# Sample attention of a hybrid decoder: both batches of a pair in one array pass, keys and values of both in one load

## The chip, the core and the metric

The kernel runs on one core of one Trainium2 chip. The metric is the time of one execution on the device in microseconds (us): the median of several runs. A profiled execution gives the trace from which the views below come; its span is the time from the first to the last instruction of the program.

## The reference

One step of a decoder layer for a prompt of 2048 tokens and for 8 running samples with 8 new tokens each. Both go through the same input projection, an attention group, an SSD group (Mamba-2), an output projection and a squared-ReLU MLP; all in f32. The change is in the attention of the samples. Each new token attends to its window buffer of 2048 cached keys and to the new keys, in three dilated groups which are combined by their log-sum-exp:

```python
def dilated_group_sample(q, k_ext, v_ext, dilation, n_keys, n_past):
    t = q.shape[1]
    idx = n_past + jnp.arange(t)[:, None] - dilation * jnp.arange(n_keys + 1)[None, :]
    valid = idx >= 0
    idx = jnp.maximum(idx, 0)
    kg, vg = k_ext[:, idx], v_ext[:, idx]
    scores = jnp.einsum('btkgd,btjkd->btkgj', q, kg, preferred_element_type=jnp.float32)
    scores = jnp.where(valid[None, :, None, None, :], scores, NEG_BIG)
    lse = jax.nn.logsumexp(scores, axis=-1)
    p = jnp.exp(scores - lse[..., None])
    o = jnp.einsum('btkgj,btjkd->btkgd', p.astype(vg.dtype), vg)
    return o, lse
```

There are 8 query heads on 4 key-value heads of 64 features, so 64 query rows (8 heads times 8 tokens) for each sample.

## The kernel before, in words

The program first does the projections and the prompt's attention, then, from about a third of the span on, the output projection (`out`, tile ps_o) and the MLP (`up`, ps_up; `down`, ps_dn) of four tiles T of 512 prompt tokens. Each f32 product of the MLP is made of three matmuls (L1124, L1126, L1127): the weight tile `raw_m` is loaded by SP (L896), split by ACT into `wm_h` (L899) and by DVE into `wm_l` (L900). There are 4 `raw` buffers and 6 of each half.

Beside tile T's MLP runs the preparation of tile T + 1, a generator (`work`) that is stepped by a plan: `tick` is called once for each `down` step, and PLAN[T] says how many steps of the generator must be done by then. For T = 1 these are the SSD work of tile 2 and then the sample attention (`sample_att`), in 26 planned steps. The generator only records instructions; a scheduler with a simulated clock then sets the order in which each engine gets them, and the engines take their instructions in that order. Copies of the key and value caches to the outputs (`shift`) run on SP too.

`sample_att` goes over 4 pairs of samples (bp). The 1280 cached keys that any of the three groups uses are gathered on the host into `kTs` (features on partitions) and `vTs` (keys on partitions); the mask `sk` holds the logarithm of how often a key counts. A pair has 128 query rows: sample be = 0 in rows 0 to 63, be = 1 in rows 64 to 127, and within a sample the two head pairs pr in 32 rows each. Its steps:

- scores (tile ps_ss): for each be, in chunks of 512, 512 and 256 keys and for each pr, a load `kts` (L1531, 3 buffers) and a matmul (L1534) with the 32 query rows as weights, so that the result lies in 32 PSUM partitions and takes 32 columns of the array; the last chunk has the 8 new keys `kn` too (L1536). DVE adds the mask and writes `Sx` (L1538), 64 partitions at a time;
- softmax over all 128 rows: maximum (L1541), exp on ACT (L1542), sum (L1544);
- transposes of the weights into 11 blocks PT (tile ps_pt, L1554);
- values (tile ps_po): for each be, five loads `vts` of two key blocks (L1566, 2 buffers) and ten matmuls (L1568), each with the 64 columns of PT of that sample as weights and 256 value features moving, then one with the new values `vn` (L1570). All add up in 64 partitions of one PSUM bank;
- the result is scaled (L1573), transposed (ps_ao, L1576) and copied into `mixA`.

The generator yields six times for a pair.

Of the kernel before, what the change touches and what calls it, by code (L numbers as in the profile page):

```python
# [9 lines left out]
F32 = mybir.dt.float32  # L10
F32R = mybir.dt.float32r
AF = mybir.ActivationFunctionType
ALU = mybir.AluOpType
# [4 lines left out]
P = 128  # L18
# [5 lines left out]
DB, DT = 8, 8  # L24
# [9 lines left out]
NEWP = 1280  # L34
# [72 lines left out]
def build(nc, tc, ctx, I, O, dbg=None, stop=None):  # L107
# [595 lines left out]
    def att_b(G_, T):  # L703
# [11 lines left out]
        for grp, A in enumerate(T.A):  # L715
            V, dV = (T.V1, T.dV1) if grp == 0 else (T.V2, T.dV2)
            for half in range(2):
# [23 lines left out]
                for prev in (0, 1):  # L741
                    for e in range(2):
# [743 lines left out]
def sample_att(nc, tc, I, O, psm, ident, qs_s, ks_s, smx, kn_s):  # L1486
    NT = DB * DT
    with ExitStack() as cx:
        sp = cx.enter_context(tc.tile_pool(name="smp", bufs=1, reuse_waits="tile"))
        mix = sp.tile([P, 4, NT], F32, name="mixA")  # L1490

        qz = sp.tile([P, 2, DB, 2, 2, DT], F32, name="qz")
        nc.vector.memset(qz, 0.0)
        kn = sp.tile([P, 2, NT], F32, name="kn")
# [8 lines left out]
        sk = sp.tile([P, NEWP + DT], F32, name="sk")  # L1503
# [11 lines left out]
        mixa = mix.rearrange("p (a j) n -> p a j n", a=2)  # L1515
        for bp in range(DB // 2):
            Sx = sp.tile([P, NEWP + DT], F32, tag="Sx", name="Sx", bufs=1)
            V = []
            for be in range(2):
                b = 2 * bp + be  # L1520
                vn = sp.tile([DT, 256], F32, tag="vn", name="vn", bufs=2)
                nc.sync.dma_start(vn, O["vnew"][b * DT:(b + 1) * DT])
                V.append(vn)
                r0 = 64 * be
                for n0 in range(0, NEWP + DT, 512):
                    n1 = min(n0 + 512, NEWP + DT)
                    ps = psm("ps_ss")
                    m1 = min(n1, NEWP)
                    for pr in range(2):
                        kt = sp.tile([P, 512], F32, tag="kts", name="kts", bufs=3)  # L1530
                        nc.sync.dma_start(kt[:, :m1 - n0], I["kTs"][b][:, pr, n0:m1])  # L1531
                        lq = qz[:, pr, b].rearrange("p e j t -> p (e j t)")
                        o = ps[r0 + 32 * pr:r0 + 32 * pr + 32]
                        nc.tensor.matmul(o[:, :m1 - n0], lq, kt[:, :m1 - n0], start=True, stop=True, skip_group_check=True)  # L1534
                        if n1 > NEWP:
                            nc.tensor.matmul(o[:, m1 - n0:n1 - n0], lq, kn[:, pr, b * DT:(b + 1) * DT], start=True, stop=True,  # L1536
                                             skip_group_check=True)
                    nc.vector.tensor_tensor(Sx[r0:r0 + 64, n0:n1], ps[r0:r0 + 64, :n1 - n0], sk[r0:r0 + 64, n0:n1], op=ALU.add)  # L1538
                yield
            mx = sp.tile([P, 1], F32, tag="mx", name="mx", bufs=1)  # L1540
            nc.vector.tensor_reduce(mx, Sx, axis=AX.X, op=ALU.max, negate=True)  # L1541
            nc.scalar.activation(Sx, Sx, AF.Exp, bias=mx)  # L1542
# [3 lines left out]
            NK = NEWP // P  # L1546
            PT = []
            for q0 in range(0, NK + 1, 4):
                q1 = min(q0 + 4, NK + 1)
                ps = psm("ps_pt")  # L1550
                pt_ = sp.tile([P, q1 - q0, P], F32, tag="PT", name="PT", bufs=3)
                for q in range(q0, q1):
                    w = P if q < NK else DT
# [5 lines left out]
                    nc.scalar.activation(pt_[:DT, NK - q0], ps[:DT, (NK - q0) * P:(NK - q0 + 1) * P], AF.Copy)  # L1559
            yield  # L1560
            po = psm("ps_po")
            for be in range(2):
                o = po[64 * be:64 * be + 64, :256]
                for j in range(5):
                    v = sp.tile([P, 2, 256], F32, tag="vts", name="vts", bufs=2)
                    nc.sync.dma_start(v, I["vTs"][2 * bp + be][:, 2 * j:2 * j + 2])  # L1566
                    for q in range(2):
                        nc.tensor.matmul(o, PT[2 * j + q][:, 64 * be:64 * be + 64], v[:, q], start=j + q == 0, stop=False,  # L1568
                                         skip_group_check=True)
                nc.tensor.matmul(o, PT[NK][:DT, 64 * be:64 * be + 64], V[be], start=False, stop=True, skip_group_check=True)  # L1570
                yield
            ao = sp.tile([P, 256], F32, tag="ao", name="ao", bufs=1)
            nc.scalar.activation(ao, po[:, :256], AF.Copy, scale=dn)  # L1573
            pt = psm("ps_ao")
# [55 lines left out]
def mix_rows():  # L1630
    a = np.arange(512).reshape(2, 2, 2, 64).transpose(0, 2, 1, 3).ravel()
    return np.concatenate([a, 512 + np.arange(512)])
# [21 lines left out]
def prep(x):  # L1654
    x = {n: np.asarray(a) for n, a in x.items()}
    A = {}
# [6 lines left out]
    w = x["w_in"][0]  # L1663
# [12 lines left out]
    j = np.arange(P)  # L1676
# [8 lines left out]
    idx, A["sk"] = sample_keys()  # L1685
    ck, cv_ = x["cache_k"][0].reshape(DB, 2048, 256), x["cache_v"][0].reshape(DB, 2048, 256)
    A["ck"], A["cv"] = ck, cv_
    A["kTs"] = ck[:, idx].reshape(DB, NEWP, 2, P).transpose(0, 3, 2, 1)
    A["vTs"] = cv_[:, idx].reshape(DB, NEWP // P, P, 256).transpose(0, 2, 1, 3)
    A["wout"] = mtiles(x["w_out"][0][mix_rows()], slice(None))  # L1690
    xr = np.zeros((KT, P, 8, NB2), np.float32)
    xr[:, :, :, :BS] = xpT.reshape(KT, P, 8, BS)
# [48 lines left out]
```

## Time and profile before

| | |
|---|---|
| median of 3 runs | 2750.95 us (2749.98 to 2755.09) |
| profiled execution | 2750.84 us |
| its span | 2749.1 us |
| outside the span | 1.7 us |
| mean granted TensorE clock | 0.978 |
| sample attention, first to last row on TensorE | 1643 to 1992 us |

In the views, PE is TensorE, PEld its weight loads, DVE VectorE, ACT ScalarE, POOL GpSimd, SP SyncE, and SPq the queue of instructions on SP that issue loads. A timeline row gives start, duration, engine, line, operation, out<-in, the rows and columns of the array in use (128\*32 is 128 rows, 32 columns), partitions x elements, and how many of them stand behind each other. Durations of matmuls overlap, since they are pipelined: what one costs is read from start to start. An f32 matmul stands as two records. A row of the chain of waits has start, duration and what the chain went through. A row of the waits has the waiting engine and line, the releaser, the total, the number of times and the longest.

### The profile page before, as it was taken

To read this page: it belongs to the slowest core of one execution; us is meant where nothing else is said; L and a number is where in the kernel's file an instruction comes from. 1 tells how busy PE (TensorE), PEld (TensorE's weight loads), DVE (VectorE), ACT (ScalarE), POOL (GpSimd) and SP (SyncE) were. 2 spreads that over 40 slices of the span, in tenths; PEclk is the share of its full clock that TensorE was granted. 3 is DMA by queue.
4 is the path that set the end of the run, shared out by engine and by line. 5 is a ranking of instruction groups with operands and counts; after the bars stand their busy time and mean duration, and the time that the engine had idled before them with its cause. 6 is when DMAs were issued, how large, how long until landed. Compare 5 with 4: busy or idle time off the path is not lost.

```text
span 2749.1 us, 42001 instructions
## 1 busy us (share of the span) xinstructions
PE 2630.7 (96%) x15318; PEld 2284.9 (83%) x15318; DVE 1660.8 (60%) x2921; ACT 1146.1 (42%) x2203; POOL 474.3 (17%) x406
## 2 busy tenths in 40 slices
PE   7999789989956999999999999999999999999998
PEld 7999789989955778888888876666688889999998
DVE  6444356887677546777467874444487764554555
ACT  5444235465543424544444442333254434333333
POOL 2222034645522100110201100020010003000000
PEclk9999899999987999999999999999999999999999
DMA  7766767886693635443574544456464434533332
GB/s 258 200 210 214 207 203 214 232 241 196 216 251 99 191 128 174 152 150 119 165 234 153 159 158 147 147 191 209 123 201 146 153 103 153 165 101 108 105 99 85
DMA packets 343327, 464.57 MB, mean 169 GB/s; under 512 B 39744, under 2 KB 219392, under 8 KB 342080
## 3 DMA queue, kind: packets, MB, share of 16 engines
q1 hardware_dynamic: 299376, 425.24, 50.2%
q10 hardware_dynamic: 43744, 36.65, 4.1%
q8 instruction: 121, 1.98, 0.3%
q14 instruction: 86, 0.70, 0.1%
HBM read 366.25 MB, written 129.09 MB: 180 GB/s over the span
## 4 chain that ended last, share of the span: by engine, by line
PE 70%; DMA 1%; DVE 1%; issue 1%; ACT 1%; POOL 0%; SPq 0%; DVEq 0%; ACTq 0%; POOLq 0%
PE ps_dn L1124 9%; PE ps_dn L1126 9%; PE ps_up L1126 9%; PE ps_dn L1127 9%; PE ps_up L1124 9%; PE ps_up L1127 9%; PE ps_o L1126 2%; PE ps_o L1124 2%; PE ps_o L1127 2%; PE ps_po L1568 1%; PE ps_ss L1534 1%; PE ps_xz L177 1%; PE ps_xz L180 1%; PE ps_xz L181 1%; PE ps_yo L1003 1%
## 5 line engine op out<-in xcount | busy, mean ns | idle before, releaser
L899 ACT ACTIVATE wm_h<-raw_m 128x512 fp32r<-128x512 f32 x576 | 362.2, 630 | 840.1 <-PE ps_dn L1126 480.8
L900 DVE TENSOR_TENSOR wm_l<-raw_m,wm_h 128x512 fp32r<-128x512 f32 x576 | 415.8, 724 | 117.1 <-ACT wm_h L899 105.0
L1124 PE MATMUL ps_dn<-uh,wm_h 128*128 128x512 f32 (+1 forms) x1280 | 458.5, 359 | 0.0
L1124 PE MATMUL ps_up<-xh_m,wm_h 128*128 128x512 f32 (+1 forms) x1280 | 458.0, 358 | 0.0
L1126 PE MATMUL ps_dn<-ul,wm_h 128*128 128x512 f32 (+1 forms) x1280 | 457.1, 357 | 0.0
L1126 PE MATMUL ps_up<-xl_m,wm_h 128*128 128x512 f32 (+1 forms) x1280 | 456.4, 357 | 0.0
L1127 PE MATMUL ps_dn<-uh,wm_l 128*128 128x512 f32 (+1 forms) x1280 | 456.0, 357 | 0.0
L1127 PE MATMUL ps_up<-xh_m,wm_l 128*128 128x512 f32 (+1 forms) x1280 | 455.5, 356 | 0.0
L1244 DVE TENSOR_TENSOR acc<-acc,ps_dn 128x512 f32<-128x512 f32 (+1 forms) x320 | 189.2, 592 | 242.6 <-PE ps_dn L1127 239.4
L1124 PEld LDWEIGHTS ps_dn<-uh,wm_h 128*128 128x128 f32 x1280 | 240.3, 188 | 43.5 <-issue 11.0
L1126 PEld LDWEIGHTS ps_dn<-ul,wm_h 128*128 128x128 f32 x1280 | 240.4, 188 | 39.0 <-issue 6.5
L1127 PEld LDWEIGHTS ps_dn<-uh,wm_l 128*128 128x128 f32 x1280 | 240.5, 188 | 37.5 <-issue 4.1
L1126 PEld LDWEIGHTS ps_up<-xl_m,wm_h 128*128 128x128 f32 x1280 | 240.8, 188 | 37.1 <-issue 4.5
L1127 PEld LDWEIGHTS ps_up<-xh_m,wm_l 128*128 128x128 f32 x1280 | 241.1, 188 | 35.4 <-issue 2.0
L1124 PEld LDWEIGHTS ps_up<-xh_m,wm_h 128*128 128x128 f32 x1280 | 240.9, 188 | 34.3 <-issue 1.2
L1232 DVE SCALAR_TENSOR_TENSOR r<-ps_up,rs 128x512 f32<-128x512 f32 (+1 forms) x160 | 95.5, 597 | 141.0 <-PE ps_up L1127 139.7
L177 PE MATMUL ps_xz<-xq,wh 128*128 128x256 f32 (+1 forms) x512 | 149.1, 291 | 12.9 <-DMA xq<-xn_s 8.2
L1235 DVE TENSOR_TENSOR ul<-r,uh 128x512 fp32r<-128x512 f32 (+1 forms) x160 | 97.0, 606 | 93.0 <-ACT uh L1234 93.0
L180 PE MATMUL ps_xz<-xq,wh 128*128 128x256 f32 (+1 forms) x512 | 148.3, 290 | 0.0
L181 PE MATMUL ps_xz<-xq,wl 128*128 128x256 f32 (+1 forms) x512 | 147.8, 289 | 0.0
L1233 ACT ACTIVATE r<-r 128x512 f32<-128x512 f32 (+1 forms) x160 | 88.8, 555 | 115.1 <-DVE r L1232 114.3
L609 PE MATMUL ps_qk<-qt,kA 128*128 128x256 f32 x300 | 103.5, 353 | 21.3 <-DMA qt<-q_s 14.0
(356 smaller groups left out, 5209.2 us busy)
## 6 DMA issues: line engine op xcount, KB each, us to landing
raw_m<-wup SPq DMA_DIRECT2D x256, 256.0 KB
raw_m<-wdn SPq DMA_DIRECT2D x256, 256.0 KB
xq<-xn_s SPq DMA_DIRECT2D x48, 512.0 KB
am<-o_s SPq DMA_DIRECT2D x128, 128.0 KB
raw_m<-wout SPq DMA_DIRECT2D x64, 256.0 KB
ks<-ck SPq DMA_DIRECT2D x32, 510.0 KB
vs<-cv SPq DMA_DIRECT2D x32, 510.0 KB
xz_s<-ev ACTq DMA_DIRECT2D x96, 128.0 KB
```

Of the source, the lines that this page charges most:

```text
L177: r = nc.tensor.matmul(ps, wh(kk), xh(kk), start=kk == 0, stop=False)
L180: nc.tensor.matmul(ps, wh(kk), xl(kk), start=False, stop=False)
L181: k.zl = nc.tensor.matmul(ps, wl(kk), xh(kk), start=False, stop=kk == KT - 1)
L609: k.mm = nc.tensor.matmul(ov, kt[:, ksl], mv, start=first, stop=False, skip_group_check=True)
L899: k.at["ACT"] = nc.scalar.activation(hi, raw, AF.Copy)
L900: nc.vector.tensor_tensor(lo, raw, hi.bitcast(F32), op=ALU.subtract)
L1124: behind(nc.tensor.matmul(ps, wh[:, kk], xh(kk), start=first and kk == 0, stop=False), after)
L1126: nc.tensor.matmul(ps, wh[:, kk], xl(kk), start=False, stop=False)
L1127: r = nc.tensor.matmul(ps, wl[:, kk], xh(kk), start=False, stop=last and kk == nk - 1)
L1232: nc.vector.scalar_tensor_tensor(r, ps, 0.0, c(X.rs), op0=ALU.max, op1=ALU.mult)
L1235: nc.vector.tensor_tensor(c(ul), r, c(uh).bitcast(F32), op=ALU.subtract)
L1244: k.at["DVE"] = nc.vector.tensor_tensor(h, h, ps, op=ALU.add)
```

## The change

Scores: the two samples of a pair are done chunk by chunk together, five chunks of 256 keys. A `kts` tile holds the chunk for both be and both pr (2 x 2 x 256 columns, 512 KB, one load, 2 buffers), and its four matmuls stand behind each other, with results in the four 32-partition strips of one ps_ss bank. The new keys are added after the last chunk. DVE adds the mask for all 128 partitions at once. Values: `vTs` is laid out by pairs, a `vts` tile holds one key block of both samples (256 KB as before), and the two matmuls of a tile are those of be = 0 and be = 1 for the same key block, with weights in columns 0 to 63 and 64 to 127 and results in two halves of one bank. `vn` of both samples comes in one load into one buffer. The generator still yields six times for a pair. In the changed kernel the lines are L1525 (load kts), L1530 (scores), L1537 (new keys), L1558 (transposes), L1568 (load vts), L1570 (values), L1575 (new values).

```diff
@@ scores @@
-            V = []
-            for be in range(2):
-                b = 2 * bp + be
-                vn = sp.tile([DT, 256], F32, tag="vn", name="vn", bufs=2)
-                nc.sync.dma_start(vn, O["vnew"][b * DT:(b + 1) * DT])
-                V.append(vn)
-                r0 = 64 * be
-                for n0 in range(0, NEWP + DT, 512):
-                    n1 = min(n0 + 512, NEWP + DT)
-                    ps = psm("ps_ss")
-                    m1 = min(n1, NEWP)
+            vn = sp.tile([DT, 2, 256], F32, tag="vn", name="vn", bufs=1)
+            nc.sync.dma_start(vn, O["vnew"].rearrange("(p e t) d -> p t e d", e=2, t=DT)[bp])
+            KC = 256
+            for n0 in range(0, NEWP, KC):
+                last = n0 + KC == NEWP
+                ps = psm("ps_ss")
+                kt = sp.tile([P, 2, 2, KC], F32, tag="kts", name="kts", bufs=2)
+                nc.sync.dma_start(kt, I["kTs"][bp, :, :, :, n0:n0 + KC])
+                for be in range(2):
                     for pr in range(2):
-                        kt = sp.tile([P, 512], F32, tag="kts", name="kts", bufs=3)
-                        nc.sync.dma_start(kt[:, :m1 - n0], I["kTs"][b][:, pr, n0:m1])
-                        lq = qz[:, pr, b].rearrange("p e j t -> p (e j t)")
-                        o = ps[r0 + 32 * pr:r0 + 32 * pr + 32]
-                        nc.tensor.matmul(o[:, :m1 - n0], lq, kt[:, :m1 - n0], start=True, stop=True, skip_group_check=True)
...
+                        lq = qz[:, pr, 2 * bp + be].rearrange("p e j t -> p (e j t)")
+                        o = ps[64 * be + 32 * pr:64 * be + 32 * pr + 32]
+                        nc.tensor.matmul(o[:, :KC], lq, kt[:, be, pr], start=True, stop=True, skip_group_check=True)
...
-                    nc.vector.tensor_tensor(Sx[r0:r0 + 64, n0:n1], ps[r0:r0 + 64, :n1 - n0], sk[r0:r0 + 64, n0:n1], op=ALU.add)
-                yield
+                w = KC + DT if last else KC
+                nc.vector.tensor_tensor(Sx[:, n0:n0 + w], ps[:, :w], sk[:, n0:n0 + w], op=ALU.add)
+                if n0 == 2 * KC:
+                    yield
+            yield
@@ values @@
+            for q in range(NK):
+                v = sp.tile([P, 2, 256], F32, tag="vts", name="vts", bufs=2)
+                nc.sync.dma_start(v, I["vTs"][bp, q])
+                for be in range(2):
+                    nc.tensor.matmul(po[64 * be:64 * be + 64, :256], PT[q][:, 64 * be:64 * be + 64], v[:, be], start=q == 0,
+                                     stop=False, skip_group_check=True)
+                if q == 4:
+                    yield
             for be in range(2):
-                o = po[64 * be:64 * be + 64, :256]
-                for j in range(5):
-                    v = sp.tile([P, 2, 256], F32, tag="vts", name="vts", bufs=2)
-                    nc.sync.dma_start(v, I["vTs"][2 * bp + be][:, 2 * j:2 * j + 2])
-                    for q in range(2):
-                        nc.tensor.matmul(o, PT[2 * j + q][:, 64 * be:64 * be + 64], v[:, q], start=j + q == 0, stop=False,
-                                         skip_group_check=True)
-                nc.tensor.matmul(o, PT[NK][:DT, 64 * be:64 * be + 64], V[be], start=False, stop=True, skip_group_check=True)
-                yield
+                nc.tensor.matmul(po[64 * be:64 * be + 64, :256], PT[NK][:DT, 64 * be:64 * be + 64], vn[:, be], start=False,
+                                 stop=True, skip_group_check=True)
+            yield
@@ prep @@
-    A["kTs"] = ck[:, idx].reshape(DB, NEWP, 2, P).transpose(0, 3, 2, 1)
-    A["vTs"] = cv_[:, idx].reshape(DB, NEWP // P, P, 256).transpose(0, 2, 1, 3)
+    A["kTs"] = ck[:, idx].reshape(DB // 2, 2, NEWP, 2, P).transpose(0, 4, 1, 3, 2)
+    A["vTs"] = cv_[:, idx].reshape(DB // 2, 2, NEWP // P, P, 256).transpose(0, 2, 3, 1, 4)
```

Where the scheduler puts the instructions then is shown by rows of TensorE's order. The end of batch pair 0's values, before (L1568 value blocks, L1570 new values; the numbers behind the names tell buffers apart):

```order
L1568 MATMUL ps_po_16889<-vts_16906,PT_16862 64x256 x2
L1570 MATMUL ps_po_16889<-vn_16589,PT_16862 64x256
L1568 MATMUL ps_po_16889<-vts_16931,PT_16848 64x256 x2
L1124 MATMUL ps_dn_17458<-uh_17291,wm_h_17454 128x512
L1126 MATMUL ps_dn_17458<-ul_17292,wm_h_17454 128x512
```

and after:

```order
L1570 MATMUL ps_po_16879<-vts_16932,PT_16852 64x256 x2
L1126 MATMUL ps_dn_17594<-ul_17314,wm_h_17590 128x512
L1570 MATMUL ps_po_16879<-vts_16936,PT_16852 64x256 x2
L1575 MATMUL ps_po_16879<-vn_16589,PT_16852 64x256 x2
L1127 MATMUL ps_dn_17594<-uh_17313,wm_l_17591 128x512
```

Before, a vts tile brings two key blocks of one sample, and the samples follow each other; after, a tile's two matmuls are the two samples of one key block. The keys at the start of pair 1, before (L1576 transposes the result of pair 0, L1534 are the scores):

```order
L1576 MATMUL ps_ao_16954<-ident_60,ao_16952 128x128 x2
L1534 MATMUL ps_ss_16984<-kts_16985,qz_16540 32x512
L1534 MATMUL ps_ss_16984<-kts_16988,qz_16540 32x512
L1534 MATMUL ps_ss_16992<-kts_16993,qz_16540 32x512
L1126 MATMUL ps_dn_17785<-ul_17336,wm_h_17781 128x512
```

and after:

```order
L1582 MATMUL ps_ao_16944<-ident_60,ao_16942 128x128 x2
L1530 MATMUL ps_ss_16974<-kts_16975,qz_16540 32x256 x4
L1530 MATMUL ps_ss_16982<-kts_16983,qz_16540 32x256 x4
L1127 MATMUL ps_dn_17703<-uh_17269,wm_l_17700 128x512
L1124 MATMUL ps_dn_17703<-uh_17313,wm_h_17699 128x512
```

Before, each matmul has a key tile of its own; after, four have one.

More of the change, by code (lines that the diff above doesn't have):

```diff
@@ new lines, in sample_att @@
+            vn = sp.tile([DT, 2, 256], F32, tag="vn", name="vn", bufs=1)
[7 more added lines that the diff above has]
+                for be in range(2):
+                    for pr in range(2):
+                        lq = qz[:, pr, 2 * bp + be].rearrange("p e j t -> p (e j t)")
+                        o = ps[64 * be + 32 * pr:64 * be + 32 * pr + 32]
+                        nc.tensor.matmul(o[:, :KC], lq, kt[:, be, pr], start=True, stop=True, skip_group_check=True)
+                if last:
+                    for be in range(2):
+                        for pr in range(2):
+                            b = 2 * bp + be
+                            lq = qz[:, pr, b].rearrange("p e j t -> p (e j t)")
+                            o = ps[64 * be + 32 * pr:64 * be + 32 * pr + 32]
+                            nc.tensor.matmul(o[:, KC:KC + DT], lq, kn[:, pr, b * DT:(b + 1) * DT], start=True, stop=True,
+                                             skip_group_check=True)
+                w = KC + DT if last else KC
+                nc.vector.tensor_tensor(Sx[:, n0:n0 + w], ps[:, :w], sk[:, n0:n0 + w], op=ALU.add)
+                if n0 == 2 * KC:
+                    yield
@@ L1561, in sample_att @@
             po = psm("ps_po")
-            for be in range(2):
-                o = po[64 * be:64 * be + 64, :256]
-                for j in range(5):
-                    v = sp.tile([P, 2, 256], F32, tag="vts", name="vts", bufs=2)
-                    nc.sync.dma_start(v, I["vTs"][2 * bp + be][:, 2 * j:2 * j + 2])
-                    for q in range(2):
-                        nc.tensor.matmul(o, PT[2 * j + q][:, 64 * be:64 * be + 64], v[:, q], start=j + q == 0, stop=False,
-                                         skip_group_check=True)
-                nc.tensor.matmul(o, PT[NK][:DT, 64 * be:64 * be + 64], V[be], start=False, stop=True, skip_group_check=True)
-                yield
+            for q in range(NK):
+                v = sp.tile([P, 2, 256], F32, tag="vts", name="vts", bufs=2)
+                nc.sync.dma_start(v, I["vTs"][bp, q])
+                for be in range(2):
+                    nc.tensor.matmul(po[64 * be:64 * be + 64, :256], PT[q][:, 64 * be:64 * be + 64], v[:, be], start=q == 0,
+                                     stop=False, skip_group_check=True)
+                if q == 4:
+                    yield
+            for be in range(2):
+                nc.tensor.matmul(po[64 * be:64 * be + 64, :256], PT[NK][:DT, 64 * be:64 * be + 64], vn[:, be], start=False,
+                                 stop=True, skip_group_check=True)
+            yield
             ao = sp.tile([P, 256], F32, tag="ao", name="ao", bufs=1)
```

2 lines of the change are left out of this document (removed).

## The prediction

> **What bounds the kernel now.** I read the page first: what each engine does over the whole span and which chain ended last.
>
> ```profile
> span 2749.1 us, 42001 instructions
> PE 2630.7 (96%) x15318; PEld 2284.9 (83%) x15318; DVE 1660.8 (60%) x2921; ACT 1146.1 (42%) x2203; POOL 474.3 (17%) x406
> PE   7999789989956999999999999999999999999998
> PE 70%; DMA 1%; DVE 1%; issue 1%; ACT 1%; POOL 0%; SPq 0%; DVEq 0%; ACTq 0%; POOLq 0%
> ```
>
> TensorE is busy for 96% of the span, and from slice 14 on every slice but the last shows a 9. But a busy share is an average, so I looked at the stretch in which the sample attention runs (its first row is at 1643, its last at 1992), first for all engines, then for the three lines alone that make the matmuls of the MLP and the output projection (MLP matmuls below).
>
> ```profile
> 1640.00:1990.00 350.00, 350.00 (x1465) 236.47 (x1465) 154.21 (x245) 109.45 (x184) 21.06 (x18) 1.00 0.53 169
> 1643.50:1992.00 348.50, 143.36 (x357) 67.06 (x357) 1.00 0.52 167
> 1643.50:1992.00 348.50, 143.72 (x356) 66.91 (x356) 1.00 0.52 167
> 1643.50:1992.00 348.50, 142.49 (x357) 67.02 (x357) 1.00 0.52 167
> ```
>
> In the first row the columns are the stretch, then PE, weight loads, DVE, ACT and POOL, the clock and the DMA share: TensorE is busy in all of the 350.00 us at full clock, DVE in 154, ACT in 109, and the DMA engines in 0.53. The other rows (L1124, L1126, L1127) count 1070 MLP matmuls in 348.5 us. How long one of them takes when nothing stands between is seen from a run of 20, of which these are the first and the last start:
>
> ```profile
> 1652.40 0.39 PE L1126 MATMUL ps_dn<-ul,wm_h 128*128 128x512 f32 x1
> ...
> 1656.84 0.40 PE L1127 MATMUL ps_dn<-uh,wm_l 128*128 128x512 f32 x1
> ```
>
> 19 steps in 4.44 us are 0.233 us each (the durations overlap, so I count from start to start). 1070 of them fill 249.3 us. The other 99 us of TensorE's time are the sample attention and a few small norm and transpose matmuls. That is the sum from which the change can take. Last, who waits:
>
> ```profile
> SPq L1531 <- PE ps_ss L1534: 39.4, 23, 4.1
> SPq L1566 <- PE ps_po L1568: 30.6, 30, 2.7
> ACT wm_h L899 <- PE ps_dn L1126: 100.8, 35, 5.7
> ACT wm_h L899 <- DMA raw_m<-wdn: 3.3, 2, 2.0
> ```
>
> The load queue waits for TensorE (a free buffer), and ACT, which splits the MLP weights, waits for TensorE 100.8 us and for a weight load 3.3 us. So the loads run ahead, and TensorE's own time is what ends last. A microsecond taken from it here is a microsecond of the span.
>
> **The change part by part.** The work on TensorE, as the trace counts it:
>
> ```profile
> L1534 PE MATMUL ps_ss<-kts,qz x96: 379/592/617, 1648.0 to 1936.4; 128*32 128x512 f32 x64, 128*32 128x256 f32 x32
> L1568 PE MATMUL ps_po<-vts,PT x160: 379/379/430, 1692.0 to 1986.2; 128*64 128x256 f32 x160
> L1570 PE MATMUL ps_po<-vn,PT x16: 374/400/425, 1708.7 to 1986.8; 8*64 8x256 f32 x16
> ```
>
> The loops issue 48 key matmuls and 80 value matmuls; the rows count 96 and 160, so an f32 matmul is two passes. A key pass uses 32 of the 128 columns of the array, a value pass 64.
>
> *What one interruption costs.* A lone key matmul among MLP matmuls, and a value group:
>
> ```profile
> 1665.18 0.40 PE L1127 MATMUL ps_dn<-uh,wm_l 128*128 128x512 f32 x1
> 1665.51 1.05 PE L1534 MATMUL ps_ss<-kts,qz 128*32 128x512 f32 x2
> 1666.48 0.50 PE L1124 MATMUL ps_dn<-uh,wm_h 128*128 128x512 f32 x1
> 1666.82 0.39 PE L1126 MATMUL ps_dn<-ul,wm_h 128*128 128x512 f32 x1
> ...
> 1707.73 1.08 PE L1568 MATMUL ps_po<-vts,PT 128*64 128x256 f32 x4
> 1708.74 0.64 PE L1570 MATMUL ps_po<-vn,PT 8*64 8x256 f32 x2
> 1709.31 1.08 PE L1568 MATMUL ps_po<-vts,PT 128*64 128x256 f32 x4
> 1710.32 0.50 PE L1124 MATMUL ps_dn<-uh,wm_h 128*128 128x512 f32 x1
> ...
> 1692.03 1.87 PE ps_po L1568 x8
> ```
>
> The key matmul takes 0.97 us until the next MLP matmul starts, and the steps into it and after it are 0.33 and 0.34 in place of 0.233: 0.20 us for each interruption. Four value passes take 1.01 us and eight (the last row, from the chain) 1.87, so one pass more costs 0.215 when it follows in the same columns. A vn matmul takes 0.57.
>
> *What a matmul in other columns costs.* This is the term that decides, and the trace has it:
>
> ```profile
> 1658.57 0.62 PE L1534 MATMUL ps_ss<-kts,qz 128*32 128x256 f32 x2
> 1659.02 0.20 PE L1536 MATMUL ps_ss<-kn,qz 128*32 128x8 f32 x2
> 1659.16 0.50 PE L1126 MATMUL ps_dn<-ul,wm_h 128*128 128x512 f32 x1
> ...
> 1677.42 0.63 PE L1534 MATMUL ps_ss<-kts,qz 128*32 128x256 f32 x4
> 1677.88 0.22 PE L1536 MATMUL ps_ss<-kn,qz 128*32 128x8 f32 x4
> 1678.03 0.50 PE L1126 MATMUL ps_dn<-ul,wm_h 128*128 128x512 f32 x1
> ...
> 1733.91 1.83 PE ps_ss L1534 x6
> ...
> 1218.61 1.09 PE L997 MATMUL ps_y<-ar,xdt 128*64 128x128 f32 x16
> 1219.63 0.82 PE L1003 MATMUL ps_yo<-cv,hst 128*128 128x128 f32 x5
> ```
>
> One 256-column key matmul with its kn takes 0.59 us; two, in two neighbouring 32-column strips, take 0.61. The second is free. The six passes at 1733.91 say the same (two matmuls in two strips, a third in the first's: 1.83, not three times 0.97), and in the SSD, whose heads lie by turns in columns 0 to 63 and 64 to 127, 16 passes take 1.02 us: 0.064 each, where 128 moving columns one after another would take half of 0.215, 0.107. So halves of 64 columns do run side by side. What no row shows is four 32-column strips at once. I bound a group of four between 0.60 (as free as the second) and 0.60 + 0.43 = 1.03 (two strips, then two), and take 0.60, to which both kinds of rows point.
>
> *Where the matmuls stand.* As the rows of TensorE's order above show, a V pair's tile is now one key block for both halves, with no MLP matmul between the two, and the keys of a tile stand four together. So it is at every place of the stage. Counting the whole order: interruptions by keys or values 65 before, 48 after (the transposes stay as they are and cancel).
>
> *Sum before.* Keys: 20 lone 512s x 0.97 = 19.4; 3 groups of three x 1.83 = 5.5; 8 groups of 256 columns x 0.59 = 4.7; 3 mixed ones, 2 x 1.40 + 0.97 = 3.8 (1.40 is 0.97 and two passes more). Values: 22 groups of four passes x 1.01 = 22.2; 9 of eight x 1.87 = 16.8; 8 vn x 0.57 = 4.6. Interruptions 65 x 0.20 = 13.0. Together 90.0 us, and with the transposes and norms that fits the 99 us counted from above.
>
> *Sum after.* Keys: 14 groups of four x 0.60 = 8.4; 3 double groups x (0.60 + 0.43) = 3.1. Values: 22 single tiles, now two passes deep, 1.01 - 0.43 = 0.58 each, 12.8; 9 of two tiles x 1.01 = 9.1; 4 vn pairs x 0.57 = 2.3 (between 0.57 and 1.14). Interruptions 48 x 0.20 = 9.6. Together 45.3 us. **The change takes 44.7 us off TensorE.**
>
> *The rest costs nothing as far as I can see.* The score additions on DVE become 20 of 128 partitions in place of 24 of 64, on an engine busy in 154 of 350 us: 0, and if DVE had no slack a saving. The loads carry the same bytes: 20 key loads of twice the size for 48, rows of 1 KB for 2 KB; 40 value loads as before; 4 vn for 8. A key load waits for the matmuls of the load two before it, and weight loads queue behind it on SP. In the order at least 98 TensorE rows, 23 us at 0.233, lie between what a key or value load waits for and the first use of a weight load queued behind it (94 before), so TensorE is not held. What is late next if a key load is late is the key matmul itself: it stands 28 to 33 rows, about 7 us, behind the release of its buffer (24 to 29 before), the value matmuls 24 to 27, about 6 us, as before. The nearest landing times in the chain of waits, both from earlier stages, are
>
> ```profile
> 769.91 3.92 DMA am<-o_s
> 794.01 7.29 DMA raw_m<-wout
> ```
>
> A key load of twice the size may take as long as two loads behind each other, 2 x 3.92 = 7.8: at worst 0.8 us at each of 12 tight ones, 10 us. I take 0, since in the old kernel three loads came into 6 us and TensorE never stood. Behind the stage TensorE is busy to the end, so nothing gives the time back there; the scheduler swaps some rows of the next stage, which I take as 0.
>
> **A rule against it.** The weight loads are hidden in the rows: the 16 passes above start 0.064 us apart, though each has a load of its own of
>
> ```profile
> L997 PEld LDWEIGHTS ps_y<-ar,xdt x256: 132/137/231, 793.2 to 2222.4; 128*64 128x64 f32 x128
> ```
>
> 0.137 us. The Trainium skill (TensorE: Matmul & The Clock Gate, Part 3: Packing small matmuls) says that a weight load overlaps running matmuls only when its row group differs, and here all tiles use all rows. By that rule the loads of the second half would lie open, the rival below with 2734.6; the trace contradicts it.
>
> **The rivals.**
> - *Two strips at a time.* Four key strips run as two pairs: 20 groups x 0.43 = 8.6 us back, 2714.7. For it: no row has four. Against: the second strip costs 0.02. Chance 0.08.
> - *Key loads late*: 10 us back, 2716.1. For it: larger loads, shorter rows, the same bytes in less time. Against: DMA share 0.53. Chance 0.07.
> - *Value halves one after another*, because both add into one PSUM bank, where the SSD's do not accumulate: 40 x 0.43 + 4 x 0.57 = 19.5 back, 2725.6. Chance 0.05.
> - *Weight loads in the open*: a value tile 2 x 0.137 more, 44 tiles with vn 12.1; a key group six loads more at no more than that, 20 x 0.82 = 16.4; 28.5 back, 2734.6. Chance 0.02.
> - *No gain*: the stage is paced by something that TensorE's full rows hide: 2751. DVE at 154 and DMA at 0.53 of the stretch speak against it. Chance 0.01.
> - *Slower: loads that land after their matmul.* All places at which a key or value load is waited for (12 tight key loads, some 20 value pairs) hold TensorE. To lose the 44.7 us and 0.2% (5.5 us) beside, each of 32 places must stand 1.6 us; the point is a landing about 7.6 us after the release, just above the longest row, 7.29. At 8 us each: 2.0 x 32 = 64, or 2770. Against: at the old kernel's 24 to 29 rows none stood. Chance 0.03.
>
> **How the numbers follow.** The profiled execution took 2750.84 us, its span 2749.1; the median of the runs is 2750.95, the same. 2750.84 - 44.7 = 2706.1. That case has a chance of 0.74 and, with a few us of swapped rows, its own range is 2700 to 2712. To 2720 the first two rivals are in: 0.89 together. From no change (0.2%, 5.5 us, is about what runs of this kernel can tell) the first five cases are far: faster 0.96, same 0.01, slower 0.03.
>
> **What would show it.** Right: TensorE still full through the stage, which is some 45 us shorter net of the MLP matmuls that move out of it; groups of key rows x8 that end within 0.6 us; value rows x4 of one tile 0.58 us from start to the next MLP matmul. Wrong: key groups of 1.0 us (two strips at a time), value tiles still at 1.01 us (no overlap), or idle TensorE ahead of key or value matmuls, released by a DMA.

## The result, and the profile after

The changed kernel takes 2705.80, 2709.68 and 2704.49 us against a median of 2751.72 us in four runs of the kernel before: a ratio of 0.9829, with a 95% interval of 0.9816 to 0.9842. (A fourth run, 3870.20 us at a granted clock of 0.604, was slow and isn't counted, nor is one slow run each of two experiments below, 7420.24 us for keys only and 4212.94 us for keys in two strips.) The forecast was 2706.1 us. The profiled execution took 2705.80 us, 45.0 less than that of before. Its page:

```profile
span 2704.1 us, 42090 instructions
PE 2582.9 (96%) x15382; PEld 2268.9 (84%) x15382; DVE 1650.8 (61%) x2917; ACT 1146.5 (42%) x2203; POOL 471.8 (17%) x406
PE 69%; DMA 3%; DVE 1%; issue 1%; ACT 0%; POOL 0%; SPq 0%; DVEq 0%; POOLq 0%; ACTq 0%
```

TensorE is still busy for 96% of the span, but for 47.8 us less of it (2582.9 for 2630.7). The chain is TensorE's as before. The stage itself, by the same rows as before: all engines, then L1124, L1126 and L1127 alone.

```profile
1643.50:1921.00 277.50, 276.84 (x1411) 199.92 (x1410) 132.81 (x216) 101.75 (x170) 21.55 (x18) 1.00 0.62 200
1643.50:1921.00 277.50, 128.23 (x319) 59.96 (x319) 1.00 0.62 200
1643.50:1921.00 277.50, 127.78 (x320) 60.01 (x319) 1.00 0.62 200
1643.50:1921.00 277.50, 127.94 (x319) 59.97 (x319) 1.00 0.62 200
```

TensorE is busy in 276.84 of 277.50 us. The stage is 71.3 us shorter than before (348.87 to 277.55, from the start of the first to the start of the last of its rows on TensorE), but only part of that is a gain: it holds 957 MLP matmuls in place of 1070 (the rows count 958, of which one had begun before the stage), and the 113 that moved out are done later. Taking 0.233 us for each, 99.6 us were left for everything else before and 54.6 after. That rest is the number to watch, in all kernels below: 45.0 us are gone from it. Rows of the new groups, from start to the next start:

```profile
1648.91 0.64 PE L1530 MATMUL ps_ss<-kts,qz 128*32 128x256 f32 x8
1649.47 0.50 PE L1124 MATMUL ps_dn<-uh,wm_h 128*128 128x512 f32 x1
1649.81 0.39 PE L1126 MATMUL ps_dn<-ul,wm_h 128*128 128x512 f32 x1
...
1680.06 1.08 PE L1570 MATMUL ps_po<-vts,PT 128*64 128x256 f32 x8
1681.07 0.50 PE L1126 MATMUL ps_up<-xl_m,wm_h 128*128 128x512 f32 x1
...
1695.63 0.39 PE L1126 MATMUL ps_up<-xl_m,wm_h 128*128 128x512 f32 x1
1695.95 0.65 PE L1570 MATMUL ps_po<-vts,PT 128*64 128x256 f32 x4
1696.53 0.50 PE L1127 MATMUL ps_up<-xh_m,wm_l 128*128 128x512 f32 x1
...
1711.97 0.65 PE L1575 MATMUL ps_po<-vn,PT 8*64 8x256 f32 x4
1712.55 0.50 PE L1127 MATMUL ps_dn<-uh,wm_l 128*128 128x512 f32 x1
...
1717.85 1.07 PE L1530 MATMUL ps_ss<-kts,qz 128*32 128x256 f32 x16
1718.85 0.50 PE L1127 MATMUL ps_dn<-uh,wm_l 128*128 128x512 f32 x1
```

Four key matmuls, eight passes, are done 0.56 to 0.57 us after they start; one alone, with its new keys, took 0.59. A value tile, four passes, takes 0.58, two tiles 1.01, a vn pair 0.58, two key groups behind each other 1.00. The steps into a group and out of it are 0.32 and 0.34, as before. Then the start of the last MLP matmul, first before, then after:

```profile
2736.99 0.30 PE L1127 MATMUL ps_dn<-uh,wm_l 128*128 128x288 f32 x1
```

```profile
2692.10 0.30 PE L1127 MATMUL ps_dn<-uh,wm_l 128*128 128x288 f32 x1
```

They are 44.89 us apart, within 0.1 us of what the rest lost: nothing behind the stage gives any of it back. The waits within the stage:

```profile
ACT wm_h L899 <- PE ps_dn L1126: 56.5, 26, 3.7
...
ACT wm_h L899 <- DMA raw_m<-wdn: 7.2, 2, 3.8
```

```profile
SPq L1568 <- PE ps_po L1570: 31.1, 24, 4.5
...
SPq L1525 <- PE ps_ss L1530: 8.9, 5, 2.7
```

The load queue still waits for TensorE to free the key and value buffers, and ACT for TensorE more than for loads. (The queue's longest wait is another, for DVE to free the buffers of MLP weights: 96.0 us, 127.4 before.) But in one place TensorE now waits for a load. It is the last key group of the third pair; first TensorE, then the load queue in order of time, then the longest wait in that queue (total, times, longest):

```profile
1801.90 0.40 PE L1127 MATMUL ps_dn<-uh,wm_l 128*128 128x512 f32 x1
1802.96 0.64 PE L1530 MATMUL ps_ss<-kts,qz 128*32 128x256 f32 x8 [0.66 <-DMA kts<-kTs]
```

```profile
1789.56 0.60 SPq L896 DMA_DIRECT2D raw_m<-wdn  x1
1795.45 0.55 SPq L1180 DMA_DIRECT2D hst<-xres  x1
1796.09 0.55 SPq L896 DMA_DIRECT2D raw_m<-wdn  x1
1796.74 0.55 SPq L1525 DMA_DIRECT2D kts<-kTs  x1
```

```profile
SPq L1180 <- DMA h_s<-hst: 7.1, 2, 5.1
```

A load of the next tile's residual (L1180) waits 5.1 us for a store to land, and the key load stands two places behind it: it is issued at 1796.74 though its buffer came free with the group at 1793.95, which is done at 1794.52. The gap is 1.06 us in place of 0.33: 0.7 us lost.

### The profile page after: what moved, and what is told of

Same layout as the page of the kernel before. It is cut to its first block, busy times and chain, and to the rows that moved or that the text cites. A ratio compares the mean times of both kernels' runs of the same rounds, so it can differ in the third digit from the quotient of the medians.

```text
span 2704.1 us, 42090 instructions
## 1 busy us (share of the span) xinstructions
PE 2582.9 (96%) x15382; PEld 2268.9 (84%) x15382; DVE 1650.8 (61%) x2917; ACT 1146.5 (42%) x2203; POOL 471.8 (17%) x406
## 4 chain that ended last, share of the span: by engine, by line
PE 69%; DMA 3%; DVE 1%; issue 1%; ACT 0%; POOL 0%; SPq 0%; DVEq 0%; POOLq 0%; ACTq 0%
PE ps_dn L1124 9%; PE ps_up L1124 9%; PE ps_up L1126 9%; PE ps_dn L1127 9%; PE ps_dn L1126 9%; PE ps_up L1127 9%; PE ps_o L1124 2%; PE ps_o L1126 2%; PE ps_o L1127 2%; PE ps_po L1570 1%; PE ps_xz L177 1%; PE ps_xz L180 1%; PE ps_xz L181 1%; PE ps_yo L1003 1%; PE ps_y L997 0%
## 5 line engine op out<-in xcount | busy, mean ns | idle before, releaser
L1124 PE MATMUL ps_up<-xh_m,wm_h 128*128 128x512 f32 (+1 forms) x1280 | 458.5, 358 | 0.0
L1124 PE MATMUL ps_dn<-uh,wm_h 128*128 128x512 f32 (+1 forms) x1280 | 458.2, 359 | 0.0
L1126 PE MATMUL ps_up<-xl_m,wm_h 128*128 128x512 f32 (+1 forms) x1280 | 456.9, 357 | 0.0
L1126 PE MATMUL ps_dn<-ul,wm_h 128*128 128x512 f32 (+1 forms) x1280 | 456.8, 357 | 0.0
L1127 PE MATMUL ps_dn<-uh,wm_l 128*128 128x512 f32 (+1 forms) x1280 | 456.6, 357 | 0.0
L1127 PE MATMUL ps_up<-xh_m,wm_l 128*128 128x512 f32 (+1 forms) x1280 | 455.4, 356 | 0.0
L1124 PEld LDWEIGHTS ps_dn<-uh,wm_h 128*128 128x128 f32 x1280 | 240.4, 188 | 37.0 <-issue 4.3
L1127 PEld LDWEIGHTS ps_dn<-uh,wm_l 128*128 128x128 f32 x1280 | 240.6, 188 | 36.7 <-issue 2.8
L1124 PEld LDWEIGHTS ps_up<-xh_m,wm_h 128*128 128x128 f32 x1280 | 241.0, 188 | 36.0 <-issue 2.7
L1127 PEld LDWEIGHTS ps_up<-xh_m,wm_l 128*128 128x128 f32 x1280 | 241.5, 189 | 35.2 <-issue 1.5
L1126 PEld LDWEIGHTS ps_up<-xl_m,wm_h 128*128 128x128 f32 x1280 | 240.9, 188 | 35.0 <-issue 2.7
L1126 PEld LDWEIGHTS ps_dn<-ul,wm_h 128*128 128x128 f32 x1280 | 240.4, 188 | 34.5 <-issue 1.5
L609 PE MATMUL ps_qk<-qt,kA 128*128 128x256 f32 x300 | 103.5, 353 | 20.9 <-DMA qt<-q_s 14.3
```

The source lines that it names most:

```text
L609: k.mm = nc.tensor.matmul(ov, kt[:, ksl], mv, start=first, stop=False, skip_group_check=True)
L1124: behind(nc.tensor.matmul(ps, wh[:, kk], xh(kk), start=first and kk == 0, stop=False), after)
L1126: nc.tensor.matmul(ps, wh[:, kk], xl(kk), start=False, stop=False)
L1127: r = nc.tensor.matmul(ps, wl[:, kk], xh(kk), start=False, stop=last and kk == nk - 1)
```

## The experiments

The whole time of a run scatters by some us, and the traces show where: the stage begins between 1640.5 and 1650.6 us in the fourteen profiles, with 2996 MLP matmuls ahead of it in every one, while from the stage's end to the last MLP matmul the three profiles of the changed kernel agree to 0.01 us (771.08, 771.09, 771.08). So I read a kernel by the rest of its stage, as defined above, and use the whole time as a second witness. The kernel before has one profile; the three of the changed kernel have rests of 53.8 to 54.6, a scatter that is nearly all one late key load (0.7, 0.5 and 0 us lost, see below).

| kernel | ratio to before, 95% | stage, us | MLP matmuls in it | rest, us |
|---|---|---|---|---|
| before | 1 | 348.87 | 1070 | 99.6 |
| after | 0.9829 (0.9816 to 0.9842) | 277.55 | 957 | 54.6 |
| after, second time | 0.9827 (0.9804 to 0.9851) | 277.31 | 957 | 54.3 |
| after, third time | 0.9821 (0.9807 to 0.9834) | 276.82 | 957 | 53.8 |
| values only | 0.9921 (0.9905 to 0.9938) | 327.94 | 1070 | 78.6 |
| keys only | 0.9906 (0.9890 to 0.9923) | 297.82 | 962 | 73.7 |
| values in the same columns | 0.9889 (0.9874 to 0.9904) | 296.81 | 964 | 72.2 |
| keys in two strips | 0.9853 (0.9834 to 0.9872) | 285.81 | 961 | 61.9 |
| values by halves | 0.9859 (0.9836 to 0.9882) | 305.59 | 1043 | 62.6 |
| larger key groups | 0.9829 (0.9806 to 0.9852) | 298.68 | 1053 | 53.3 |
| value tiles of two | 0.9824 (0.9803 to 0.9845) | 299.45 | 1071 | 49.9 |
| the same, second time | 0.9812 (0.9799 to 0.9825) | 299.45 | 1071 | 49.9 |
| both larger | 0.9791 (0.9777 to 0.9805) | 306.46 | 1108 | 48.3 |
| keys, one buffer | one run | 351.17 | 1267 | 56.0 |

The theory under test: the stage is TensorE's time, and what the change took from it is that matmuls in different columns run side by side. The main rival: the gain is that loads are merged and groups stand closer together, so it would come without the columns.

**The two parts apart.** The values part alone, on the kernel before:

```diff
-            for be in range(2):
-                o = po[64 * be:64 * be + 64, :256]
-                for j in range(5):
...
-                    nc.sync.dma_start(v, I["vTs"][2 * bp + be][:, 2 * j:2 * j + 2])
-                    for q in range(2):
...
+            for q in range(NK):
...
+                nc.sync.dma_start(v, I["vTs"][bp, q])
+                for be in range(2):
...
```

> The old kernel with the values part of the change alone: the value tiles hold one key block of both samples and their matmuls stand in the two column halves; the keys stay as they were, one load and one matmul at a time. Theory (TensorE's time counts, and the second column half is free): the 40 value tiles stand as 18 single ones of 0.58 us, 11 groups of two of 1.01, and 4 pairs of vn of 0.57, 23.8 us in place of 43.6; 62 interruptions in place of 65, 0.6 less; together 20.4 off, 2731 us. The two parts should add up: this one's gain and the keys' gain to the whole 44. Rival (the gain comes from the keys, merged loads and fewer interruptions): this kernel stays within 3 us of before, 2749 or more.

And the keys part alone:

```diff
-                for n0 in range(0, NEWP + DT, 512):
...
-                    for pr in range(2):
-                        kt = sp.tile([P, 512], F32, tag="kts", name="kts", bufs=3)
...
+            for n0 in range(0, NEWP, KC):
...
+                kt = sp.tile([P, 2, 2, KC], F32, tag="kts", name="kts", bufs=2)
...
+                for be in range(2):
+                    for pr in range(2):
...
```

> The old kernel with the keys part of the change alone: five chunks of 256 keys with four matmuls in four column strips, one load each; the values stay as they were, one sample after the other. Theory: 12 lone groups of 0.58 us and 4 double ones of 1.03 make 11.1 us in place of 33.4, and the interruptions by keys or values go from 65 to 47, 3.6 less: 25.9 off, 2726 us. Rival (four strips run as two pairs, and what the values save hides it): 20 x 0.43 less of a gain, 2734. Rival (loads of twice the size land late): over 2734, and gaps ahead of the key groups, released by a DMA.

In the trace, values alone first: a lone key matmul, as it was, and a new value tile.

```profile
1649.38 1.04 PE L1532 MATMUL ps_ss<-kts,qz 128*32 128x512 f32 x2
1650.36 0.50 PE L1124 MATMUL ps_dn<-uh,wm_h 128*128 128x512 f32 x1
...
1700.09 0.65 PE L1564 MATMUL ps_po<-vts,PT 128*64 128x256 f32 x4
1700.67 0.50 PE L1126 MATMUL ps_up<-xl_m,wm_h 128*128 128x512 f32 x1
```

Measured: the rest falls by 21.0 us for the values (20.4 expected) and by 25.9 for the keys (25.9 expected); the whole time by 21.6 (2733.17 from 2754.79) and by 24.7 (2730.12). The whole change took 45.0, 1.9 less than the two together, and the counts have 1.6 of that (20.4 + 25.9 against 44.7): the groups fall together differently in each order. Keys alone has the reverse, a new key group and an old value tile:

```profile
1654.83 0.64 PE L1534 MATMUL ps_ss<-kts,qz 128*32 128x256 f32 x8
1655.40 0.50 PE L1124 MATMUL ps_dn<-uh,wm_h 128*128 128x512 f32 x1
...
1694.10 1.08 PE L1576 MATMUL ps_po<-vts,PT 128*64 128x256 f32 x4
1695.11 0.50 PE L1124 MATMUL ps_up<-xh_m,wm_h 128*128 128x512 f32 x1
```

Eight key passes in 0.57 us stand beside four value passes in 1.01. Neither part leans on the other, and the rival that gave the gain to the keys alone is out.

**The columns taken away from the values.** Same loads, same number and order of value matmuls, but both samples in columns 0 to 63:

```diff
-                    nc.tensor.matmul(po[64 * be:64 * be + 64, :256], PT[q][:, 64 * be:64 * be + 64], v[:, be], start=q == 0,
-                                     stop=False, skip_group_check=True)
+                    nc.tensor.matmul(po[:64, 256 * be:256 * be + 256], PT[q][:, 64 * be:64 * be + 64], v[:, be],
+                                     start=q == 0 and be == 0, stop=False, skip_group_check=True)
...
-            nc.scalar.activation(ao, po[:, :256], AF.Copy, scale=dn)
+            nc.scalar.activation(ao[:64], po[:64, :256], AF.Copy)
+            nc.scalar.activation(ao[64:], po[:64, 256:], AF.Copy)
+            nc.scalar.activation(ao, ao, AF.Copy, scale=dn)
```

> The changed kernel, but the value matmuls of both samples have their weights in the same columns, 0 to 63, with results side by side in one bank (256 and 256 columns); same loads, same number of matmuls; the scaling takes three ACT copies in place of one. Theory (the gain of the values is the second column half): 16 single tiles go back to 1.01 us, 12 groups of two to 1.87, 4 vn pairs to 1.14: 43.2 in place of 24.1, less 3 interruptions (0.6): 18.5 slower than the changed kernel, 2726 us. Rival (the gain is the new order and the loads by pairs): as the changed kernel, 2706 to 2709.

```profile
1680.28 1.94 PE L1570 MATMUL ps_po<-vts,PT 128*64 128x256 f32 x8
1682.15 0.50 PE L1126 MATMUL ps_up<-xl_m,wm_h 128*128 128x512 f32 x1
...
1696.05 1.08 PE L1570 MATMUL ps_po<-vts,PT 128*64 128x256 f32 x4
1697.06 0.50 PE L1124 MATMUL ps_up<-xh_m,wm_h 128*128 128x512 f32 x1
```

A tile is back at 1.01 and two at 1.87. The rest rises by 17.6 to 18.4 us (from 54.6, the first profile of after, or 53.8, its third, which had no late load; this kernel's profile has one late key load too, 0.5 us lost), 18.5 expected, and the ratio to 0.9889. The loads by pairs and the new order are all still there, and the values' gain is gone: it was the second half of the columns.

**Two strips for four.** The key matmuls of the second sample in the strips of the first, its results in the second half of the bank:

```diff
-                        o = ps[64 * be + 32 * pr:64 * be + 32 * pr + 32]
-                        nc.tensor.matmul(o[:, :KC], lq, kt[:, be, pr], start=True, stop=True, skip_group_check=True)
+                        o = ps[32 * pr:32 * pr + 32, KC * be:KC * be + KC]
+                        nc.tensor.matmul(o, lq, kt[:, be, pr], start=be == 0, stop=True, skip_group_check=True)
...
```

> The changed kernel, but the four key matmuls of a chunk lie in two column strips only, two behind each other in each, the second sample's result in the second half of the bank; the mask is then added in two instructions of 64 partitions and one ACT copy. Theory (each strip is a place of its own, and four cost what one costs): a lone group goes from 0.57 to 0.57 + 0.43 = 1.00 us, 20 x 0.43 = 8.6 slower, 2716 us. Rival (not the strips but the standing together and the one load make the keys' gain): no change, 2706 to 2709. Rival (the wider mask additions on DVE count too): above 2719.

```profile
1647.18 1.06 PE L1529 MATMUL ps_ss<-kts,qz 128*32 128x256 f32 x8
1648.16 0.50 PE L1124 MATMUL ps_dn<-uh,wm_h 128*128 128x512 f32 x1
```

0.98 us for the same eight passes that took 0.57 in four strips, and 7.3 to 8.1 us more in the rest, for 8.6 expected (two interruptions fewer, 46 for 48, take 0.4 of that back). Four strips are four places. The mask additions, more than twice as many here (44 for 20, with 20 copies on ACT), cost nothing that can be seen.

**Side by side, or by turns?** So far a matmul that ran beside another stood right behind it. Here two tiles are done as sample 0, sample 0, sample 1, sample 1:

```diff
-            for q in range(NK):
+            for q0 in range(0, NK, 2):
...
                 for be in range(2):
-                    nc.tensor.matmul(po[64 * be:64 * be + 64, :256], PT[q][:, 64 * be:64 * be + 64], v[:, be], start=q == 0,
-                                     stop=False, skip_group_check=True)
+                    for q in range(q0, q0 + 2):
+                        nc.tensor.matmul(po[64 * be:64 * be + 64, :256], PT[q][:, 64 * be:64 * be + 64], vv[q - q0][:, be],
+                                         start=q == 0, stop=False, skip_group_check=True)
```

> The changed kernel, but the value matmuls of two tiles are written in the order sample 0, sample 0, sample 1, sample 1, in place of by turns; same loads, same columns. In the order they then stand as 16 lone matmuls, 16 groups of three and 4 of four, and the interruptions by keys or values go from 48 to 53. Theory (a matmul in the other columns is free only when it stands right behind one in the first): 16 x 0.58 + 16 x 1.01 + 4 x 1.45 + 4 vn x 0.57 = 33.5 us in place of 24.2, and 5 x 0.20: 10.3 slower than the changed kernel. A variant of it (TensorE looks past a matmul that waits for its columns): the groups of four take 1.01 in place of 1.45, 8.6 slower. Rival (a column half has work of its own for as long as the tiles are there, whatever the order): within 2 us of the changed kernel.

The order of a group of four on TensorE, by the tiles' numbers (tile 16880 for sample 0, 16882 for sample 0, then both for sample 1), and below it such a group, then a lone matmul, in the trace:

```
L1574 MATMUL ps_po_16879<-vts_16880,PT_16838 64x256
L1574 MATMUL ps_po_16879<-vts_16882,PT_16838 64x256
L1574 MATMUL ps_po_16879<-vts_16880,PT_16838 64x256
L1574 MATMUL ps_po_16879<-vts_16882,PT_16838 64x256
```

```profile
1678.92 1.09 PE L1574 MATMUL ps_po<-vts,PT 128*64 128x256 f32 x8
1679.94 0.50 PE L1126 MATMUL ps_up<-xl_m,wm_h 128*128 128x512 f32 x1
...
1686.88 0.65 PE L1574 MATMUL ps_po<-vts,PT 128*64 128x256 f32 x2
1687.45 0.50 PE L1124 MATMUL ps_up<-xh_m,wm_h 128*128 128x512 f32 x1
```

The group of four takes 1.02 us, what it takes by turns, not 1.45. The rest rises by 8.0 to 8.8 us: 8.6 was the variant in which TensorE looks past a matmul that waits for its columns, 10.3 the strict order. So my first theory fell and its variant holds. What costs the 8 us is not the order inside a group but that 16 matmuls were left alone: one takes 0.57 us, as long as two in different columns. The rival "whatever the order" is out by the same rows.

**Larger key groups.** Chunks of 512, 512 and 256 keys, 1 MB a load, one buffer:

```diff
-            KC = 256
+            KC = 512
...
-                kt = sp.tile([P, 2, 2, KC], F32, tag="kts", name="kts", bufs=2)
+                kt = sp.tile([P, 2, 2, KC], F32, tag="kts", name="kts", bufs=1)
...
```

> The changed kernel with key chunks of 512, 512 and 256 in place of five of 256, the loads twice as large (1 MB) and one buffer in place of two, since two don't fit. Theory (only TensorE's time counts, and strips stay free with 512 columns): 8 groups of 512 x 0.97 and 4 of 0.61 make 10.2 us in place of 11.4, the interruptions go from 48 to 46, and the value tiles stand as 28 single and 6 double groups, 0.5 more: about 1.1 faster than the changed kernel. Rival (with one buffer the load of a chunk starts only when the last matmul of the chunk before is done, and lands late): gaps ahead of the key groups, released by a DMA, at 1 to 5 us each for 12 groups, 10 to 60 slower.

```profile
1655.61 1.07 PE L1531 MATMUL ps_ss<-kts,qz 128*32 128x512 f32 x8
1656.60 0.50 PE L1126 MATMUL ps_dn<-ul,wm_h 128*128 128x512 f32 x1
```

Four strips with 512 columns take 0.99 us, two groups of 256 behind each other 1.00. The rest is 0.5 to 1.3 us less, 1.1 expected; the whole time can't show that (0.9829 for 0.9827). TensorE never waits for a key load: the key groups of a pair stand 8 to 14 us apart.

**Value tiles of two.** Two key blocks of both samples in a load of 512 KB, one buffer, so that two tiles always stand together:

```diff
-            for q in range(NK):
-                v = sp.tile([P, 2, 256], F32, tag="vts", name="vts", bufs=2)
-                nc.sync.dma_start(v, I["vTs"][bp, q])
+            for q0 in range(0, NK, 2):
+                v = sp.tile([P, 2, 2, 256], F32, tag="vts", name="vts", bufs=1)
+                nc.sync.dma_start(v, I["vTs"][bp, q0:q0 + 2].rearrange("q p e d -> p q e d"))
...
```

> The changed kernel with two key blocks of both samples in one value tile: 20 loads of 512 KB and one buffer in place of 40 loads of 256 KB and two buffers, the same memory. Theory (what is left to take is the lone tiles and the interruptions): 20 groups of 1.01 us in place of 22 of 0.58 and 9 of 1.01, 1.7 less; keys 0.2 less; 36 interruptions in place of 48, 2.4 less: 4.3 faster than the changed kernel. Rival (one buffer): the loads land late, with gaps ahead of the value groups, released by a DMA; at 0.3 us each for 20 groups the gain is gone.

The rest falls by 3.9 to 4.7 us, 4.3 expected, and no load is late; but the whole time was 2706.06 us for 2707.69, which settles nothing. So it ran again with more rounds, beside the changed kernel and the next kernel.

> The changed kernel once more, unaltered, beside the next three on the same chip, since chips differ by some us: 0.983 of before, between 0.9815 and 0.9845; a gap of about 0.7 us ahead of the key group of the third pair that holds the new keys, if its late load in the first profile was no accident.

> Value tiles of two key blocks once more, with more rounds, beside the changed kernel on the same chip. The stage alone was 4.7 us shorter in its first profile, the whole time 1.6 us, with profiles whose stage began up to 7 us apart. Theory (the stage's gain is a gain of the whole, and the rest is the scatter ahead of the stage): 4 to 5 us under the changed kernel, 0.1815 to 0.1825 per cent of it or a ratio to before that is 0.0016 lower, and 50.1 us in the stage. Rival (something behind the stage gives it back): the stage at 50.1 again, and the stretch from the stage's end to the last MLP matmul longer by as much for the same number of MLP matmuls.

> The changed kernel, unaltered, as the measure for the next two on the same chip: 0.983 of before; the time of the stage that is not MLP matmuls 54.5 to 54.8 us, as in its two profiles.

(The percentage in the second of these is a slip; 4 to 5 us are 0.15 to 0.18% of the time.) The stage came out at 299.45 us both times, to the last digit. The whole time was 2702.49 us for 2705.83, 3.3 less, but with intervals that overlap. Behind the stage 4573 MLP matmuls take 744.57 us (1942.11 to 2686.68) and 744.71 us (1946.95 to 2691.66) in the two profiles, and in the kernel before 4574 take 744.81 (1992.18 to 2736.99): nothing is given back behind the stage, as the rival had it. By the trace the stage's gain is the whole's; the whole time by itself is too scattered to show 4 us. As to the late load: 0.7 us in the first profile of after, 0.5 in the second, none in the third.

**Both larger.** Key chunks of 512 and value tiles of two together, the edits of the last two kernels:

> Key chunks of 512, 512 and 256 and value tiles of two key blocks together, each with one buffer. Theory (a group costs 0.20 us for the interruption, and what stands in it costs its passes in the fullest columns): 8 x 0.98 + 4 x 0.61 = 10.3 us of keys in place of 11.4, 20 x 1.01 = 20.2 of values in place of 21.9, 32 interruptions in place of 48 (3.2 less): 6.0 less than the changed kernel, 48.6 us in the stage, and 0.002 lower as a ratio to before, if no load is late. Rival (single buffers, 1 MB and 512 KB loads on one queue): gaps ahead of key and value groups, released by a DMA, that sum to 6 us or more: no gain over the changed kernel.

```profile
1647.72:1954.16 306.44, 147.40 (x369) 69.38 (x369) 1.00 0.59 195
1647.72:1954.16 306.44, 146.70 (x370) 69.38 (x369) 1.00 0.59 195
1647.72:1954.16 306.44, 147.04 (x370) 69.54 (x370) 1.00 0.59 195
```

By these rows (L1124, L1126, L1127; 1109, of which one had begun before the stage) 1108 MLP matmuls fill 258.2 of the stage's 306.46 us, and the rest is 48.3: 5.5 to 6.3 less than after, 6.0 expected. The time is 2697.67 us (2694.74 to 2703.74) for 2705.83 of the changed kernel beside it, and the intervals of the two ratios don't touch: 0.9777 to 0.9805 for 0.9807 to 0.9834. This is the fastest version here. No load is late.

**One key buffer.** What the second buffer is worth:

```diff
-                kt = sp.tile([P, 2, 2, KC], F32, tag="kts", name="kts", bufs=2)
+                kt = sp.tile([P, 2, 2, KC], F32, tag="kts", name="kts", bufs=1)
```

> The changed kernel with one buffer for the key chunks of 256 in place of two, so that a load starts only behind the matmuls of the chunk before: the price of the cover that the prediction counted on. In the order the 20 key groups then stand alone, and the values as 28 single and 6 double tiles; interruptions 54 in place of 48. Theory (the order puts MLP matmuls enough between a release and the next group, so the loads stay hidden): 1.2 for the interruptions, 0.8 for the groups, 2.0 more in the stage than the changed kernel, 56.7 us. Rival (two buffers hid the loads): gaps ahead of most key groups, released by a DMA, 1 us or more each for 16 groups, over 70 us in the stage.

The rest is 56.0, 1.4 to 2.2 more than after, for 2.0 expected, and no group waits for its load. Its one run took 2714.70 us, but its stage also began 7.1 us later than that of after (1650.58 for 1643.47), so the whole time isn't read. The scheduler pays for the missing buffer by spacing a pair's key groups about 8 to 9 us apart, and the spacing costs lone groups, not waits.

## Why the prediction was right, point by point

- **The bound.** TensorE's time: shown. The rests of nine altered kernels, from 21 us less than before to 6 less than after, came out within 1.3 us of a count of TensorE's groups alone, while loads, buffers, ACT copies and DVE additions changed with them.
- **Interruptions, 0.20 each, 48 for 65.** The steps are 0.32 and 0.34, so 0.20 holds.
- **Keys, 33.4 to 11.5.** Measured from the groups: 10 of 0.57, 4 of 0.61 and 3 double ones of 1.00 make 11.1. Four strips at the price of one, the value I chose from 0.60 to 1.03, was right, and "two strips at a time" is out: that is what the kernel with two strips does, at 0.98.
- **Values, 43.6 to 24.2.** 22 of 0.58, 9 of 1.01 and 4 vn pairs of 0.58 make 24.2. The 43.6 is some 0.4 too low: it counts three places where new values stand between two value tiles as a double tile of 1.87 and a vn of 0.57, while the prediction's own rows show 1.01, 0.57 and 1.01 there (1707.73 to 1710.32). "Value halves one after another", the reason given for it being the shared bank that both add into, is out: the shared bank is still there, and the tiles take 0.58.
- **Weight loads in the open.** Out. The weight loads of the key group at 1648.91 are one row beside the group's first passes, all eight of them begun and done within 0.16 us, while one takes 0.106 to 0.109:

```profile
1648.90 0.16 PEld L1530 LDWEIGHTS ps_ss<-kts,qz 128*32 128x32 f32 x8 [0.37 <-issue]
```

  The Trainium skill (TensorE: Matmul & The Clock Gate, Part 3: Packing small matmuls) has a weight load overlap running matmuls only when its row group differs; here all rows are the same and only the columns differ, so the row speaks against it.
- **Loads, 0 with 10 us at worst.** 0.7, 0.5 and 0 us in three profiles. The forecast was right in size, but its working left a case out: it looked at what queues behind a key load on SP, and not at what a key load queues behind. The late load of the first profile was held up by a wait ahead of it on the queue, and ahead of that of the second the same residual load waits as long, 5.2 us.
- **Order swaps behind the stage, 0.** The last MLP matmul is 44.89 us earlier, so yes.
- **DVE, 0.** The additions take 8.1 us for 14.3 in the stage, and TensorE's weight loads waited for them once, 0.4 us; the kernel with more than twice as many shows no price either.
- **The slower rival**, every load late by 2 us, did not come near: with one buffer, or with 1 MB in a load, no key group waited at all.

The sum was 44.7; the profiles show 45.0. The agreement to 0.3 us is partly luck. The sum left out 0.4 us of gain in the values and 0.4 in the keys, and the late load, which it took as 0, gave 0.7 of them back in the profile of the result; without a late load the rest is 53.8 and the gain nearly 46. The start of the stage scatters by more than all of this. That start's scatter lies ahead of everything changed here, and its cause stays open.

## What to carry to other kernels

When TensorE is full, look for matmuls that use few columns and give their partners other columns: here two half-width matmuls cost what one costs, and four quarter-width ones too. Count the groups as well as the passes, since each group among other matmuls cost 0.20 us, and a lone matmul the same 0.57 us as a filled set of columns; larger loads paid only by making such groups (6 us here). Where the whole time scatters, subtract the bulk work from the stage that was changed, and compare that.

## What the runs showed of the hardware that was not expected

TensorE does not keep to its order across columns. In the group of four written sample 0, sample 0, sample 1, sample 1, the first two records start 13 ns apart (1678.923 and 1678.936), and the group ends after 1.02 us. By turns, the first two start 7 ns apart (1695.949 and 1695.956). A lone matmul shows how passes follow each other in the same columns: its second starts 0.267 us behind its first (1686.876 and 1687.143). So the record 13 ns behind must belong to sample 1, whose first matmul is the third instruction: it overtook the second. The records don't name their columns, but they say which of them raise a semaphore, and that bears it out: in all four such groups these are the fourth record, 0.28 us behind the first, and the eighth. In the program the third and the fourth matmul raise it, each as the last reader of its tile; in the written order their last passes would be the sixth record and the eighth. So the first four records are the two passes of the first and of the third matmul, and the second matmul begins only with the fifth, 0.48 us behind the group's start. The Trainium skill (TensorE: Matmul & The Clock Gate, Part 3: Packing small matmuls) says that matmuls are strictly first in, first out, with no reordering. By that the group would have taken at least about 1.45 us (an estimate: the 1.01 us of a group by turns and two more passes of 0.215), and it didn't.
